# Other dense tiles, tokens paced at fewer bytes per ns in the front, and dense weights loaded two expert blocks per transfer

## The chip, the cores and the metric

The kernel runs on one core of a Trainium2 chip. The metric is the device time of one execution in microseconds (us), lower is better. A change of less than 0.3% (12 us) cannot be told from no change. Engines are named as in the profile: PE (matrix products), PEld (its weight loads), DVE (vector), ACT (activations), POOL (which issues the gathers here) and SP (which issues most transfers); a "q" behind a name is the engine's queue of instructions.

## The reference, cut to what matters

One decoder block over 1024 tokens of width 1024. A front of three attention branches, gates and projections gives `x`; then every token picks 128 of 16,384 experts (8 heads, 16 each) and mixes them:

```python
h2 = rms_norm(x, g_ffn)
q  = (hf @ w_q).reshape(T, 8, 2, 128)
sc = einsum('thpd,hpkd->thpk', q, subkeys)        # two times 128 scores a head
...                                               # top 16 of each, top 16 of the 256 sums: idx, gate
act = gelu(einsum('chkd,cd->chk', u[ic], hc))     # u, v: (16384, 1024) float32
w   = gate * act
out = einsum('chk,chkd->cd', w, v[ic])
x   = x + out
```

## The kernel before, in words

**Tiles and groups.** The 1024 tokens are eight tiles of 128. The front (`phase1`) works on four groups of two tiles, in order: norm, stick-breaking attention, dilated attention, memory attention, `gating` (24 gate blocks and their branch projections), `out_proj`, `ffn_norm`, `select` (the scores) and, as a side job, `topk`, which turns the scores of one tile at a time into expert numbers and gates. All its weights stream from HBM in blocks of 512 KB (`Weights.prepare`, tile `w`, at most four in flight).

**Two ways through the experts.** Six tiles are done by gathers (`experts`): for each token POOL issues one indirect transfer (L983) that fetches the 128 rows `[u | v]` that it picked, 8 KB a row and 1 MB a token, into one of eight buffers `uv`. DVE forms the 128 inner products (L994) against the token's row, spread over partitions by a matmul (L989), and sixteen small matmuls a token (L1015) sum the v rows into `po`. The two tiles in `DENSE` go another way: `gate_matrix` builds a full matrix of gates (128 x 128 experts a token) by one-hot products, stores it to `gd`, and at the end `dense` runs all 16,384 experts for these 256 tokens, in 128 blocks of 128 experts. A block loads `u` (512 KB, tile `ur`), `v` (512 KB, tile `vr`) and every fourth time a piece of `gd` (tile `g`, 512 KB in runs of 512 bytes); `split` makes a rounded part on ACT and the rest on DVE (L1095); 24 matmuls give the activations, ACT and DVE apply gelu and gate, and after every second block (`C = 2`) 24 matmuls bring the result through `v` and DVE adds it to `acc` (L1137). `ur`, `vr`, `uh`/`ul` and `vh`/`vl` have two buffers each.

**The order of the work** is fixed at build time by a planner at the end of `block_kernel`. The front and the dense part are one long generator (`rest`, called filler); each `yield` is a step. The planner keeps two clocks, `pe` and `dma`, in ns. A token adds `TOKEN_NS` (700) to `pe` and `TOKEN_BYTES / BW` to `dma`; a step of filler adds its matmul cost (the `cost` sums in `mm`, `mmr` and `flip`, and 50 ns) times `SLOW` (1.38 in the front, 1.1 in the dense part) to `pe` and its loaded bytes divided by `BW` to `dma`. Before each token it lays down steps of filler until `pe` has reached `dma`. Where no tile is ready (`ready` is empty) it lays down filler alone, and tokens alone where the filler is used up. A tile becomes ready when `topk` is through; a dense tile gives no tokens. All engines take their instructions in the order so laid down.

The gate matrix of a dense tile is built in the `gating` and `out_proj` steps of later groups (`stage` 1, 56 steps a group), so many of its steps with each step of the front; at `stage` 2, behind `out_proj`, all that is left of it is laid down at once. A tile takes 83 of its steps, 64 of them with work.

Of the kernel before, what the change touches and what calls it, by code (L numbers as in the profile page):

```python
# [7 lines left out]
F32 = mybir.dt.float32  # L8
# [3 lines left out]
AF = mybir.ActivationFunctionType  # L12
# [5 lines left out]
D = 1024  # L18
T = 1024
NT = T // 128  # L20
KD = D // 128
# [6 lines left out]
F32R = mybir.dt.float32r  # L28
MANUAL = dict(engines={mybir.EngineType.Activation})
GROUPS = (2, 2, 2, 2)  # L30
DENSE = (4, 5)
ND = len(DENSE)
GATES = len(GROUPS) - 1
PAUSE = 4
RG = 3
LAG = 1


BW = 375.0
SLOW = 1.38, 1.1  # L40
TOKEN_NS, TOKEN_BYTES = 700.0, 128 * 8192 + 3 * 8192.0
LEAST = 3000.0
# [32 lines left out]
def block_kernel(ctx: ExitStack, tc: tile.TileContext, io):  # L75
    nc = tc.nc
# [23 lines left out]
    cost = [0.0]  # L100
    moved = [0.0]
    table = [None]

    def bank():
        return ps.tile([128, 512], F32, name="bank")
# [8 lines left out]
    def flip(out, in_):  # L114
        cost[0] += 120
        nc.tensor.transpose(out, in_, ident)

    def actf(out, in_, f, **kw):
        s = SETS.get(f)
        if s and table[0] != s:  # L120
            nc.scalar.preload_act_table_set(s)  # L121
            table[0] = s
        nc.scalar.activation(out, in_, f, **kw)  # L123
# [111 lines left out]
    def count(ap):  # L235
        n = 4.0
        for d in ap.shape:
            n *= d
        moved[0] += n

    def load(out, src):
        count(out)
        nc.sync.dma_start(out, src)
# [486 lines left out]
    def ffn_norm(x2, n0, G, h2T):  # L730
# [26 lines left out]
        for i, h2 in enumerate(h2s):  # L757
            n = n0 + i
            if n in DENSE:
                nc.scalar.dma_start(h2d[DENSE.index(n)], h2T[:, :, i * 128:(i + 1) * 128])  # L760

            for part in range(3 if n not in DENSE else 0):
                b = gw.tile([128, D], BF, name="part", bufs=2)
# [43 lines left out]
    def topk(n0, G, scs, out):  # L807
        for i in range(G):
# [63 lines left out]
            pt = bank()  # L872
            if n0 + i in DENSE:
                flip(pt[:, 0:128], sel[:, 0, :])
# [3 lines left out]
                actf(st, pt[:, :384].rearrange("p (a b) -> p a b", a=3), AF.Copy)  # L878
                nc.scalar.dma_start(seld[DENSE.index(n0 + i)], st)
                stored.append(n0 + i)  # L880
# [143 lines left out]
    def mmr(out, lhsT, rhs, **kw):  # L1024
        cost[0] += rhs.shape[-1] / 2.4 + 3
        nc.tensor.matmul(out, lhsT, rhs, **kw)  # L1026
# [45 lines left out]
    C = 2  # L1072

    def dense():
        st = ctx.enter_context(ExitStack())
        dp = st.enter_context(tc.tile_pool(name="dp", bufs=2))
        hh = dp.tile([128, KD, TD], F32R, name="hh", bufs=1)
        hl = dp.tile([128, KD, TD], F32R, name="hl", bufs=1)
        acc = dp.tile([128, ND, D], F32, name="acc", bufs=1)
        for i in range(ND):  # L1080
            r = dp.tile([128, KD, 128], F32, name="ur")
            load(r, h2d[i])
            c = slice(i * 128, (i + 1) * 128)
            actf(hh[:, :, c], r, AF.Copy)
            nc.vector.tensor_sub(hl[:, :, c], r, hh[:, :, c])
            load(acc[:, i, :], xres[DENSE[i]])
        yield

        def split(src, name, bufs):
            r = dp.tile([128, D], F32, name=name + "r")  # L1090
            load(r, src)
            hi = dp.tile([128, D], F32R, name=name + "h", bufs=bufs)
            lo = dp.tile([128, D], F32R, name=name + "l", bufs=bufs)
            actf(hi, r, AF.Copy)
            nc.vector.tensor_sub(lo, r, hi)  # L1095
            return hi, lo

        us, vs, ws = {}, {}, {}
        gt = {}
        us[0] = split(io["uT"][0], "u", 2)  # L1100
        for c in range(128 // C):
            for x in range(C):
                e = c * C + x
                if e % 4 == 0:
                    gt = dp.tile([128, TD // 32, 4, 32], F32, name="g")
                    load(gt, gd[:, :, e:e + 4, :].rearrange("b p i t -> p b i t"))
                if e + 1 < 128:
                    us[e + 1] = split(io["uT"][e + 1], "u", 2)
                vs[x] = split(io["v"][e], "v", C)
                uh, ul = us.pop(e)  # L1110
                a = bank()
                for k in range(KD):
                    kc = slice(k * 128, (k + 1) * 128)
                    mmr(a[:, :TD], uh[:, kc], hh[:, k, :], start=k == 0, stop=False)
                    mmr(a[:, :TD], ul[:, kc], hh[:, k, :], start=False, stop=False)
                    mmr(a[:, :TD], uh[:, kc], hl[:, k, :], start=False, stop=k == KD - 1)
                w = dp.tile([128, TD], F32, name="w")
                actf(w, a[:, :TD], AF.Gelu)
                nc.vector.tensor_mul(w.rearrange("p (b t) -> p b t", t=32),
                                     w.rearrange("p (b t) -> p b t", t=32), gt[:, :, e % 4, :])  # L1120
                wh = dp.tile([128, TD], F32R, name="wh", bufs=C)
                wl = dp.tile([128, TD], F32R, name="wl", bufs=C)
                actf(wh, w, AF.Copy)
                nc.vector.tensor_sub(wl, w, wh)  # L1124
                ws[x] = wh, wl
                yield
            for i in range(ND):
                for half in range(2):
                    o = bank()
                    f = slice(half * 512, (half + 1) * 512)  # L1130
                    for x in range(C):
                        wh, wl = (z[:, i * 128:(i + 1) * 128] for z in ws[x])
                        vh, vl = (z[:, f] for z in vs[x])
                        mmr(o, wh, vh, start=x == 0, stop=False)
                        mmr(o, wh, vl, start=False, stop=False)
                        mmr(o, wl, vh, start=False, stop=x == C - 1)
                    nc.vector.tensor_add(acc[:, i, f], acc[:, i, f], o)  # L1137
                    yield
        for i in range(ND):
            nc.sync.dma_start(io["out"][DENSE[i]], acc[:, i, :])  # L1140
# [3 lines left out]
    def sides(n):  # L1144
        while n and side:
            if next(side[0], 0) == 0:
                side.pop(0)
            n -= 1
# [3 lines left out]
    def rest():  # L1152
        n0 = built = 0
        for g in range(len(GROUPS)):
            for stage in phase1(g, n0, GROUPS[g], ready):
                if stage and built < ND:

                    want = sum(n < n0 for n in DENSE)
                    while len(stored) < want:
                        sides(1)  # L1160
                    for _ in range(999 if stage == 2 else RG if g == GATES else 2):
                        if built < want:
                            built = next(gates)
                yield
            n0 += GROUPS[g]
        front.close()
        slow[0] = SLOW[1]
        yield from dense()

    filler = [rest()]  # L1170
    slow = [SLOW[0]]
    pe = dma = due = 0.0

    def fill(nside):

        c, m = cost[0], moved[0]
        if next(filler[0], 0) == 0:
            filler[0] = None
        spent = (cost[0] - c + 50) * slow[0], (moved[0] - m) / BW
        c, m = cost[0], moved[0]  # L1180
        sides(nside)
        cost[0], moved[0] = c, m
        return spent

    done = 0
    while done < NT - ND or filler[0] is not None:
        if ready:
            for _ in experts(*ready.pop(0)):

                due = max(due + LEAST, pe - LEAST)  # L1190
                while filler[0] is not None and (dma > pe or pe < due):
                    a, b = fill(1)
                    pe += a
                    dma += b
                pe += TOKEN_NS
                dma += TOKEN_BYTES / BW
            done += 1
        else:
            a, b = fill(4)
            pe += a  # L1200
            dma = max(dma + b, pe)
# [48 lines left out]
```

## Time and profile before

| | |
|---|---|
| median of 3 runs | 3950.37 us (3945.61 to 3955.39) |
| the profiled execution, its time | 3939.4 us |
| its span from first to last instruction | 3937.6 us |
| mean granted PE clock | 0.916 |
| busy share PE / DVE / ACT / POOL | 83% / 67% / 32% / 19% |
| moved by DMA | 1243.61 MB, mean 316 GB/s |
| gathers (L983) | 768 transfers, 805.36 MB of that |

The busy shares are means over stages with different limits. The second part of the page, which cuts the span into 40 slices of 98 us, and windows cut at the stages say more; they are shown with the argument. A busy digit of 9 is 90% or more, PEclk is the granted PE clock in tenths of full speed, and the DMA row is the mean busy share of the core's 16 DMA engines.

### The profile page before, as it was taken

What the parts mean: (1) busy time and instruction counts of PE and PEld (TensorE: products, weight loads), DVE (VectorE), ACT (ScalarE), POOL (GpSimd) and SP (SyncE); (2) the same over time, 40 slices, a digit from 0 to 9 for tenths busy, and PEclk for the clock granted to TensorE, in tenths of its full rate; (3) what the DMA queues carried; (4) which work ended last, traced back from release to release, by engine and by line L of the source; (5) the groups of instructions that cost most, each with busy time, mean ns of one, the idle gap of its engine ahead of it and who ended that gap; (6) DMA issues with size and microseconds to landing.
All of it is one profiled execution on the core that took longest, in us unless ns stands there. A gap on an engine that the chain in (4) does not pass through costs nothing.

```text
span 3937.6 us, 63428 instructions
## 1 busy us (share of the span) xinstructions
PE 3287.9 (83%) x23618; PEld 2552.2 (65%) x23618; DVE 2654.0 (67%) x8133; ACT 1258.3 (32%) x2518; POOL 757.0 (19%) x776
## 2 busy tenths in 40 slices
PE   7999788888768888898888898987799999999644
PEld 6889656656645565566655567876577777777411
DVE  5443696655458696554587855646988888878755
ACT  3442434420013443200145443432233433333100
POOL 0000023222222232232223210000122121111333
PEclk9999888989979999998899999998899999999865
DMA  4445479999989999999999972554799999999998
GB/s 137 127 127 173 148 307 379 371 369 402 392 338 383 394 370 358 363 396 393 403 390 378 359 291 94 186 204 149 276 343 354 369 354 358 346 332 370 367 417 364
DMA packets 293739, 1243.61 MB, mean 316 GB/s; under 512 B 31416, under 2 KB 94392, under 8 KB 191800
## 3 DMA queue, kind: packets, MB, share of 16 engines
q0 software_dynamic: 110592, 805.36, 50.7%
q1 hardware_dynamic: 157712, 394.46, 28.3%
q10 hardware_dynamic: 25128, 39.75, 2.8%
q8 instruction: 187, 3.06, 0.3%
q14 instruction: 120, 0.98, 0.1%
HBM read 1198.68 MB, written 40.76 MB: 315 GB/s over the span
## 4 chain that ended last, share of the span: by engine, by line
PE 46%; DMA 24%; DVE 18%; issue 6%; ACT 4%; POOL 2%; ACTq 0%; POOLq 0%; SPq 0%; DVEq 0%
PE bank L112 27%; PE bank L1026 12%; DMA uv<-in_uv,iT 10%; PE po L1015 6%; DVE uv L994 5%; DMA vr<-in_v 4%; DMA w<-in_w_gate 3%; POOL uv L983 2%; DMA b3d<-part 1%; DVE vl L1095 1%; DVE acc L1137 1%; DMA h2d<-big 1%; DMA w<-in_w_in 1%; DMA w<-in_w_pq 1%; DVE ul L1095 1%
## 5 line engine op out<-in xcount | busy, mean ns | idle before, releaser
L983 POOL DMA_INDIRECT uv<-in_uv,iT x768 | 756.2, 985 | 3157.8 <-PE po L1015 1192.0
L994 DVE SCALAR_TENSOR_TENSOR uv<-uv,pb 128x512 f32<-128x512 f32 x1536 | 998.7, 680 | 336.1 <-DMA uv<-in_uv,iT 289.6
L112 PE MATMUL bank<-big,w 128*128 128x256 f32 x3072 | 747.7, 395 | 92.2 <-DMA w<-in_w_gate 50.6
L112 PEld LDWEIGHTS bank<-big,w 128*128 128x128 f32 x3072 | 592.0, 197 | 221.9 <-issue 88.7
L1015 PE MATMUL po<-uv,wz 128*32 128x256 f32 x6144 | 459.0, 442 | 55.4 <-DVE wz L1006 55.0
L1015 PEld LDWEIGHTS po<-uv,wz 128*32 128x32 f32 x6144 | 202.8, 124 | 298.2 <-DVE wz L1006 121.9
L989 PE MATMUL pb<-b,which 96*128 96x512 bf16 x384 | 156.0, 429 | 232.3 <-DVE uv L994 199.7
L1026 PE MATMUL bank<-hh,ul 128*128 128x256 f32 x1024 | 296.8, 290 | 23.7 <-DVE ul L1095 23.7
L123 ACT ACTIVATE gel<-acts 128x4 f32<-128x4 f32 x192 | 38.8, 202 | 853.1 <-DVE acts L1001 842.2
L1026 PE MATMUL bank<-hh,uh 128*128 128x256 f32 x1024 | 297.2, 290 | 15.6 <-DVE pos L773 11.4
L112 PEld LDWEIGHTS bank<-w,big 128*128 128x128 f32 x2432 | 283.4, 193 | 22.2 <-issue 17.4
L1026 PE MATMUL bank<-hl,uh 128*128 128x256 f32 x1024 | 295.3, 288 | 0.0
L112 PE MATMUL bank<-w,big 128*128 128x128 f32 x2432 | 289.7, 277 | 3.7 <-DMA w<-in_w_out 3.7
L1026 PE MATMUL bank<-vh,wh 128*128 128x512 f32 x512 | 216.2, 423 | 34.0 <-ACT wh L123 31.2
L1026 PE MATMUL bank<-uv 128*128 128x256 f32 x1632 | 223.7, 294 | 15.6 <-ACT uv L123 9.0
L1026 PEld LDWEIGHTS bank<-uv 128*128 128x128 f32 x1632 | 209.2, 197 | 21.5 <-ACT uv L123 10.3
L1026 PEld LDWEIGHTS bank<-hh,ul 128*128 128x128 f32 x1024 | 201.7, 197 | 29.4 <-DVE ul L1095 26.6
L1026 PEld LDWEIGHTS bank<-hh,uh 128*128 128x128 f32 x1024 | 201.6, 197 | 24.1 <-issue 14.8
L121 ACT ACT_TABLE_LOAD x156 | 200.1, 1283 | 42.9 <-issue 14.7
L1026 PE MATMUL bank<-vh,wl 128*128 128x512 f32 x512 | 200.3, 396 | 6.3 <-DVE wl L1124 6.3
L989 PEld LDWEIGHTS <-which 96*128 96x128 bf16 x384 | 37.0, 101 | 256.8 <-issue 249.5
L1026 PEld LDWEIGHTS bank<-hl,uh 128*128 128x128 f32 x1024 | 201.7, 197 | 1.7 <-issue 1.6
(240 smaller groups left out, 5137.9 us busy)
## 6 DMA issues: line engine op xcount, KB each, us to landing
w<-in_w_in SPq DMA_DIRECT2D x136, 512.0 KB
ur<-in_uT SPq DMA_DIRECT2D x128, 512.0 KB
vr<-in_v SPq DMA_DIRECT2D x128, 512.0 KB
w<-in_w_gate SPq DMA_DIRECT2D x96, 512.0 KB
w<-in_w_pq SPq DMA_DIRECT2D x64, 512.0 KB
w<-in_w_o SPq DMA_DIRECT2D x64, 256.0 KB
w<-in_w_out SPq DMA_DIRECT2D x32, 512.0 KB
gd<-big ACTq DMA_DIRECT2D x16, 1024.0 KB
```

The costliest lines, as they stand in the source:

```text
L112: nc.tensor.matmul(out, lhsT, rhs, **kw)
L121: nc.scalar.preload_act_table_set(s)
L123: nc.scalar.activation(out, in_, f, **kw)
L983: nc.gpsimd.indirect_dma_start(out=uv, out_offset=None, in_=io["uv"], in_offset=bass.IndirectOffsetOnAxis(ap=iT[:, c, jj, i:i + 1], axis=0))
L989: nc.tensor.matmul(pb, which[:, jj].rearrange("p q s -> p (q s)"), b3[:, hh * 512:(hh + 1) * 512], start=True, stop=True)
L994: nc.vector.scalar_tensor_tensor(uv[:, f], uv[:, f], 1.0, pb, op0=OP.mult, op1=OP.mult, accum_out=parts[:, hh, i:i + 1])
L1015: nc.tensor.matmul(po[32 * k:32 * k + 32, h:h + 256], wz[:, i, :], uvs[i][:, f], start=jj == 0 and i == 0, stop=jj == QB - 1 and i == 3, s ...
L1026: nc.tensor.matmul(out, lhsT, rhs, **kw)
L1095: nc.vector.tensor_sub(lo, r, hi)
L1137: nc.vector.tensor_add(acc[:, i, f], acc[:, i, f], o)
```

## The change

- `DENSE` is (3, 5) and no longer (4, 5): tile 3 (second of the second group) goes the dense way, tile 4 (first of the third group) is gathered.
- `BW` becomes a pair: 320 bytes per ns while the front is laid down, 380 in the dense part (it was 375 throughout).
- The gate matrix moves one step with each step of `gating` and `out_proj` in any group (it was three in the last group, two in others); the rest at `stage` 2 as before.
- `u` and `v` of the dense part are stored as 64 pairs of blocks, and one transfer brings a pair: 128 rows of 8 KB, 1 MB. `raw` loads it and `split` takes one half of it. `ur` of the next pair and `vr` of the present one are loaded at the start of a pair, ahead of `g`.

```diff
-DENSE = (4, 5)
+DENSE = (3, 5)
-GATES = len(GROUPS) - 1
-RG = 3
-BW = 375.0
+BW = 320.0, 380.0
...
-        def split(src, name, bufs):
-            r = dp.tile([128, D], F32, name=name + "r")
+        def raw(src, name):
+            r = dp.tile([128, C, D], F32, name=name)
             load(r, src)
+            return r
+
+        def split(r, x, name, bufs):
             hi = dp.tile([128, D], F32R, name=name + "h", bufs=bufs)
             lo = dp.tile([128, D], F32R, name=name + "l", bufs=bufs)
-            actf(hi, r, AF.Copy)
-            nc.vector.tensor_sub(lo, r, hi)
+            actf(hi, r[:, x], AF.Copy)
+            nc.vector.tensor_sub(lo, r[:, x], hi)
             return hi, lo
...
-        us[0] = split(io["uT"][0], "u", 2)
+        ur = {0: raw(io["uT"][0], "ur")}
+        us[0] = split(ur[0], 0, "u", 2)
         for c in range(128 // C):
+            if c + 1 < 128 // C:
+                ur[c + 1] = raw(io["uT"][c + 1], "ur")
+            vr = raw(io["v"][c], "vr")
             for x in range(C):
...
-                    us[e + 1] = split(io["uT"][e + 1], "u", 2)
-                vs[x] = split(io["v"][e], "v", C)
+                    us[e + 1] = split(ur[(e + 1) // C], (e + 1) % C, "u", 2)
+                vs[x] = split(vr, x, "v", C)
...
-                    for _ in range(999 if stage == 2 else RG if g == GATES else 2):
+                    for _ in range(999 if stage == 2 else 1):
...
-        slow[0] = SLOW[1]
+        slow[0], bw[0] = SLOW[1], BW[1]
...
-        spent = (cost[0] - c + 50) * slow[0], (moved[0] - m) / BW
+        spent = (cost[0] - c + 50) * slow[0], (moved[0] - m) / bw[0]
...
-                dma += TOKEN_BYTES / BW
+                dma += TOKEN_BYTES / bw[0]
...
-        "uT": a["peer_u"][0].reshape(128, 128, KD, 128).transpose(0, 3, 2, 1).reshape(128, 128, D),
-        "v": a["peer_v"][0].reshape(128, 128, D),
+        "uT": a["peer_u"][0].reshape(64, 2, 128, KD, 128).transpose(0, 4, 1, 3, 2)
+        .reshape(64, 128, 2, D),
+        "v": a["peer_v"][0].reshape(64, 2, 128, D).transpose(0, 2, 1, 3),
```

More of the change, by code (lines that the diff above doesn't have):

```diff
@@ L1087, in dense @@
         yield
-        def split(src, name, bufs):
-            r = dp.tile([128, D], F32, name=name + "r")
+        def raw(src, name):
+            r = dp.tile([128, C, D], F32, name=name)
             load(r, src)
+            return r
+        def split(r, x, name, bufs):
             hi = dp.tile([128, D], F32R, name=name + "h", bufs=bufs)
             lo = dp.tile([128, D], F32R, name=name + "l", bufs=bufs)
-            actf(hi, r, AF.Copy)
-            nc.vector.tensor_sub(lo, r, hi)
+            actf(hi, r[:, x], AF.Copy)
+            nc.vector.tensor_sub(lo, r[:, x], hi)
             return hi, lo
         us, vs, ws = {}, {}, {}
-        gt = {}
-        us[0] = split(io["uT"][0], "u", 2)
+        ur = {0: raw(io["uT"][0], "ur")}
+        us[0] = split(ur[0], 0, "u", 2)
         for c in range(128 // C):
+            if c + 1 < 128 // C:
+                ur[c + 1] = raw(io["uT"][c + 1], "ur")
+            vr = raw(io["v"][c], "vr")
             for x in range(C):
@@ L1166, in rest @@
         front.close()
-        slow[0] = SLOW[1]
+        slow[0], bw[0] = SLOW[1], BW[1]
         yield from dense()
     filler = [rest()]
-    slow = [SLOW[0]]
+    slow, bw = [SLOW[0]], [BW[0]]
     pe = dma = due = 0.0
```

## The prediction

> **What bounds the kernel now.** I start with the 40 slices of the page, then cut windows at the places where the POOL row changes.
>
> ```profile
> span 3937.6 us, 63428 instructions
> ...
> PE   7999788888768888898888898987799999999644
> ...
> POOL 0000023222222232232223210000122121111333
> PEclk9999888989979999998899999998899999999865
> DMA  4445479999989999999999972554799999999998
> GB/s 137 127 127 173 148 307 379 371 369 402 392 338 383 394 370 358 363 396 393 403 390 378 359 291 94 186 204 149 276 343 354 369 354 358 346 332 370 367 417 364
> ```
>
> The POOL row shows where gathers run: from slice 5 to 23, none in 24 to 27, then to the end. In the gap the DMA row falls to 2 to 5 tenths and PE stands at 7 to 9. Outside it, and behind the first group, DMA is at nine tenths. So two resources take turns at being short. The windows give the amounts:
>
> ```profile
> core 0: us, PE busy (x) PEld busy (x) DVE busy (x) ACT busy (x) POOL busy (x), PEclk, DMA share, GB/s
> 0.00:505.00 505.00, 430.83 (x3291) 396.84 (x3291) 258.87 (x734) 196.29 (x402) 0.84 (x8) 0.92 0.45 142
> 505.00:2310.00 1805.00, 1504.37 (x10944) 1087.47 (x10948) 1206.04 (x4247) 551.99 (x1087) 487.04 (x508) 0.91 0.95 378
> 2310.00:2720.00 410.00, 371.73 (x2482) 320.57 (x2474) 215.47 (x823) 144.87 (x447) 3.74 (x4) 0.96 0.45 155
> 2720.00:2900.00 180.00, 127.72 (x905) 105.64 (x906) 172.24 (x545) 60.04 (x88) 25.48 (x24) 0.86 0.75 275
> 2900.00:3690.00 790.00, 741.69 (x5193) 603.92 (x5192) 664.63 (x1345) 300.23 (x473) 156.52 (x143) 0.99 0.94 354
> 3690.00:3938.00 248.00, 111.56 (x813) 37.71 (x812) 136.79 (x449) 4.93 (x24) 83.42 (x90) 0.64 0.96 394
> ```
>
> Row by row: (1) group 0, no tile ready. (2) Fronts of groups 1, 2 and the start of 3 beside 508 gathers: DMA 0.95, PE 1504 of 1805 us. (3) The rest of group 3 alone: the 512 gathers of tiles 0 to 3 are used up, PE 372 of 410 us, DMA 0.45. (4) Top-k of the last two tiles and the start of dense, DVE 172 of 180 us. (5) Dense beside 143 gathers: PE 0.94 and DMA 0.94 at once. (6) 90 gathers alone at 394 GB/s, PE 0.45. Rows 2 and 3 are what the change is about: in one the DMA engines are full, in the next they idle. That PE really waits in row 2 is in its own waits from 600 to 2300 us:
>
> ```profile
> PE pb L989 <- DVE uv L994: 74.1, 50, 8.9
> PE bank L112 <- DMA w<-in_w_gate: 50.6, 18, 8.6
> PE po L1015 <- DVE wz L1006: 30.2, 27, 8.7
> ```
>
> Token products behind late rows, and late weights: 155 us in these three alone.
>
> **The front, by the planner.** What the new constants do to the order can be worked out from the listing. Adding up the planner's own sums step by step, the filler from the first token slot to the start of dense has 440 steps with 1376 us of matmul cost (1398 with 50 ns a step) and 186 MB, or 0.133 MB per us of filler. With f us of filler to a token both clocks agree when 700 + 1380 f = 1,073,152/BW + 133,000 f/BW. BW 375: 2162 = 1025 f, f = 2.11. BW 320: 2654 = 964 f, f = 2.75. A tile has 129 slots (one sets it up), four tiles 516. Before, 516 slots take 516 x 2.11 = 1089 us of the filler, the last 309 stay alone; stepping through gives 98 steps with 333 us, which is row 3. After, 1398/2.75 = 508 slots fit. Stepping through gives the same 508 at the start of dense and never more than a few steps without a token: tile 2 ready at slot 183 (tiles 0 and 1 last to 258), tile 4 ready at 355 (tile 2 lasts to 387). So the gap goes, by an exchange of tile 4 for tile 3 that costs nothing in gathers (512 either way).
>
> Its price needs both resources over rows 2 and 3, 2215 us together.
>
> DMA: 1805 x 0.95 + 410 x 0.45 = 1899 us of engine time, unchanged. At the 0.94 that row 5 holds beside a busy PE this is 2020 us. That is the floor.
>
> PE: a token costs it (459.0 + 156.0)/768 = 0.80 us:
>
> ```profile
> L994 DVE SCALAR_TENSOR_TENSOR uv<-uv,pb 128x512 f32<-128x512 f32 x1536 | 998.7, 680 | 336.1 <-DMA uv<-in_uv,iT 289.6
> ...
> L1015 PE MATMUL po<-uv,wz 128*32 128x256 f32 x6144 | 459.0, 442 | 55.4 <-DVE wz L1006 55.0
> ...
> L989 PE MATMUL pb<-b,which 96*128 96x512 bf16 x384 | 156.0, 429 | 232.3 <-DVE uv L994 199.7
> ```
>
> The filler alone runs in row 3: 338 us of cost (with the 50 ns) in some 405 us, 1.20 of its cost, stalls included. So 1398 x 1.20 + 508 x 0.80 = 2084 us if no stall of the filler is filled by a token's matmuls, which is the pessimistic way to add. DVE is not nearer: rows 2 and 3 hold 1422 us of it. I take 2065, between 2020 and 2084 and nearer the second, as two streams that are both nearly full wait for each other. **Front: -150 us** (2215 to 2065).
>
> Bounds: below, 1899/0.95 = 2000 (-215). Above, the filler's rate in row 1, 505 us for 390 us of cost, 1.29, though that has the start in it: 1398 x 1.29 + 406 = 2209 (-6).
>
> **The gate matrix.** Work is the same; half goes from group 3 to group 2, both in the sums above. New is the dump: 56 of 83 steps go one by one, 27 remain at stage 2, in groups 2 and 3.
>
> ```profile
> L1045 DVE TENSOR_SCALAR ab<-iota,sl 128x128 f32<-128x128 f32 x256 | 86.8, 339 | 56.2 <-PE bank L112 53.8 <-DMA sl<-seld 2.4
> ...
> L1047 DVE TENSOR_SCALAR ab<-iota,sl 128x128 f32<-128x128 f32 x256 | 71.2, 278 | 0.0
> ```
>
> A step is two of each on DVE, 1.23 us; 27 (some idle) make at most 33 us in which no token is laid down. Eight `uv` buffers at 1805/508 = 3.55 us a token cover 28 us of gathers. What sticks out is 5 us a dump: **+10** (0 to +66, if nothing covered it). SP's loads queue behind nothing new here; the two 1 MB stores a quarter tile from ACT move along, 8 MB of them from the empty stretch to a full one, in the DMA sum already.
>
> **The dense part.** Eight more slots than before lie in it (266 for 258, by stepping), two of them (98 for 96) behind its last block. Six beside dense, PE-bound, at 0.80: +5; two in the tail at 248/96 = 2.6: +5. Top-k of tile 6 now has one side step a filler step, so 20 more steps of dense start beside it; row 4 is DVE-bound either way and only exchanges order: 0. BW 380 for 375 moves the ratio by 1%, in these counts.
>
> Of the transfers the page's issues, and the queues (packets, MB, share of the engines' time) from 2950 to 3650 us:
>
> ```profile
> ur<-in_uT SPq DMA_DIRECT2D x128, 512.0 KB
> vr<-in_v SPq DMA_DIRECT2D x128, 512.0 KB
> ```
>
> ```profile
> q1 hardware_dynamic: 54300, 116.42, 47.2%
> q0 software_dynamic: 17856, 130.03, 45.9%
> ```
>
> The waits (us in total, times, longest) of ACT in the same stretch, of SP from 2900 to 3690:
>
> ```profile
> ACT uh L123 <- DMA ur<-in_uT: 37.6, 17, 8.6
> ACT vh L123 <- DMA vr<-in_v: 37.4, 26, 4.3
> ```
>
> ```profile
> SPq L243 <- DVE ul L1095: 401.6, 97, 9.1
> ```
>
> Pairs halve the issues, 256 to 128, but SP is not short: it waits 401.6 us for a split to free `ur`. On the engines, q1 moves 116.42 MB in 0.472 x 700 = 330 us, 352 GB/s; q0 (8 KB rows) 130.03 MB in 321 us, 405 GB/s. Were the 134 MB of pairs to go from the one rate to the other, 49 us of DMA time would be saved at most; much of q1's loss is `g`'s short runs, which stay. PE idles 790 - 742 = 48 us in row 5 in all, so the gain ends there: -40. Against it stands latency: a pair of `ur` and `vr` is 2 MB that SP can issue only about one pair time ahead (790/58 = 13.6 us) and that needs 2.1/(0.1664 MB per us, q1's mean) = 12.6 us, where before 1 MB had the same lead. Splits now read a half only when all has come. I take **+5** (-40 to +60, a waiting ACT costing what it does now again: 37.4 + 37.6 with some hidden).
>
> The Trainium skill, "DMA: Bandwidth & Descriptors", section "Anatomy of one DMA", says that a transfer's semaphore fires only when its last byte is confirmed in place, which speaks against pairs: by it the first half comes later by the second half's 0.5 MB, 3.2 us by q1's mean rate, and 64 pairs would lose 205 us if nothing lay ahead. The row of ACT's `vr` waits, 37.4 us in 26, shows that most loads do lie ahead.
>
> **Sum.** 3939.4 - 150 + 10 + 10 + 5 = 3814 on the profiled execution, which stands 11 us under the median of the runs shown; on that scale **3825**.
>
> **The rivals.**
>
> *Better overlap.* Tokens fill all stalls of the filler and DMA holds 0.95: front 2000, dense gains 40: 3939 - 215 + 20 - 40 + 11 = 3715. For it: row 5 shows 0.94 on both at once. Against: the front's chains through ACT and DVE are longer. PEclk is 0.91 in row 2 and 0.99 in row 5; the PE work of rows 2 and 3 at 0.97 would be 1504 x 0.91/0.97 + 372 x 0.96/0.97 = 1779 us, far from binding. The Trainium skill, "TensorE: Matmul & The Clock Gate", Part 1, says that the clock is halved after an idle window of some 3.4 us and released by sustained work; the trace agrees (0.64 in the tail with PE at 0.45), and by it the fuller front runs at the better clock, which would carry this rival.
>
> *Chain-bound front.* Filler keeps the pace of row 1, 1.29: front 2209, the total 3939 - 6 + 25 + 11 = 3969 at worst, 3886 to 3955 for 1.23 to 1.28. For it: row 2 has stretches where neither PE nor DMA is full (slice 11 at 338 GB/s, slice 15 at 358, PE 8 tenths in both). Against: row 3.
>
> *Dense starved, slower.* `ur` and `vr` of a pair, and `g` behind them (2.6 MB, 15.8 us of q1's mean, against 13.6), come late and PE stops at each pair. A stop of 2 us more a pair than my +5 is 64 x 2 = 128 and brings no change; from there it decides. At 4 us: 3825 + 256 = 4081. For it: landings of `vr` are 4% of the span (some 150 us) in the chain that ended last:
>
> ```profile
> PE bank L112 27%; PE bank L1026 12%; DMA uv<-in_uv,iT 10%; PE po L1015 6%; DVE uv L994 5%; DMA vr<-in_v 4%; DMA w<-in_w_gate 3%; POOL uv L983 2%; DMA b3d<-part 1%; DVE vl L1095 1%; DVE acc L1137 1%; DMA h2d<-big 1%; DMA w<-in_w_in 1%; DMA w<-in_w_pq 1%; DVE ul L1095 1%
> ```
>
>  Against: 48 us of PE idle in row 5 says most lateness is absorbed, and the doubled buffers hold two pairs.
>
> **How the numbers follow.** Forecast (3770 to 3885) 0.62; better overlap 0.13; chain-bound 0.16, of it 0.10 faster, 0.04 the same, 0.02 slower; starved 0.09, of it 0.02 the same, 0.07 slower. Within 0.3% is 12 us, about what a measurement here can tell. Faster 0.85, same 0.06, slower 0.09. The range 3735 to 3915 leaves out half of the better overlap and the far ends of the other two.
>
> **What would show it.** POOL without the four empty slices; DMA at 0.9 or more from 500 us to the end; PE about 0.9 and PEclk 0.94 or more there; dense starting near 2570 in place of 2720, its stage 780 to 810 us; q1's packets fewer by some 16,000 to 32,000 if rows go as 8 KB. I am wrong if the DMA share in the front falls under 0.88 (chain-bound), if ACT's waits for `vr` exceed 150 us with PE idle over 100 us in dense (starved), or if gathers still pause for want of a tile.

## The result, and the profile after

The changed kernel takes 3861.03 us (median of 4, 3856.79 to 3870.02), the kernel before beside it 3952.88: a ratio of 0.9773, interval 0.9749 to 0.9796, 92 us less. The forecast was 3825, the range 3735 to 3915. The mechanism is the one forecast, its size about seven tenths of it: the sum said 125 us less; the medians fell by 92, the spans of the two profiled executions by 83.

The slices of the changed kernel's page:

```profile
span 3855.0 us, 63108 instructions
...
PE   7999789898789989888899898877798999999644
...
POOL 0000022222122222112222221120121121121332
PEclk9999889999899989999999999888899999999755
DMA  3334479889899978999898899887798989999898
GB/s 141 128 127 170 161 291 380 317 351 376 346 357 380 377 280 331 365 380 360 319 381 351 333 364 368 327 318 282 275 357 323 386 335 371 358 353 357 354 417 358
```

The POOL row has no empty stretch any more behind slice 4; one slice, 27, is a zero, where the front ends. But the DMA row does not stand at 9 throughout: 7 and 8 come back again and again, at 275 to 358 GB/s. In windows cut at the start of dense (2605) and the same stages as before (PE, PEld, DVE, ACT and POOL busy with counts, then PEclk, DMA share, GB/s):

```profile
505.00:2605.00 2100.00, 1834.55 (x13312) 1401.10 (x13313) 1390.79 (x5009) 682.96 (x1512) 486.44 (x506) 0.94 0.89 351
2605.00:2810.00 205.00, 149.82 (x1056) 119.20 (x1056) 188.34 (x580) 65.39 (x99) 29.11 (x26) 0.86 0.73 278
2810.00:3605.00 795.00, 738.91 (x5144) 604.66 (x5142) 660.33 (x1355) 290.29 (x467) 156.22 (x146) 0.97 0.90 352
3605.00:3855.00 250.00, 112.47 (x817) 37.69 (x813) 138.66 (x452) 4.93 (x24) 84.71 (x91) 0.59 0.96 395
```

The front takes 2100 us in place of 2215 with 506 gathers in it; the start of dense 205 for 180; dense and the tail are as they were. So the front gave 115, and 32 came back between the start of dense and the end. The last row of each kernel's `acc` additions tells where that is (first and last start), before and after:

```profile
L1137 DVE TENSOR_TENSOR acc<-acc,bank x256: 662/681/690, 2746.7 to 3688.8; 128x512 f32<-128x512 f32 x128
```

```profile
L1141 DVE TENSOR_TENSOR acc<-acc,bank x256: 665/682/690, 2641.5 to 3596.6; 128x512 f32<-128x512 f32 x128
```

From the start of dense (2719 and 2605) to the first addition 27.5 and 36.5 us, from first to last 942 and 955, behind it to the end 249 and 258.

### The profile page after: what moved, and what is told of

The parts are those of the page before. It is cut to its first block, busy times and chain, and to the rows that moved or that the text cites. A ratio compares the mean times of both kernels' runs of the same rounds, so it can differ in the third digit from the quotient of the medians.

```text
span 3855.0 us, 63108 instructions
## 1 busy us (share of the span) xinstructions
PE 3263.3 (85%) x23618; PEld 2556.4 (66%) x23618; DVE 2641.3 (69%) x8133; ACT 1241.1 (32%) x2506; POOL 757.3 (20%) x776
## 3 DMA queue, kind: packets, MB, share of 16 engines
q1 hardware_dynamic: 139280, 394.45, 27.6%
## 4 chain that ended last, share of the span: by engine, by line
PE 48%; DMA 22%; DVE 13%; issue 11%; ACT 3%; POOL 2%; ACTq 0%; POOLq 0%; SPq 0%; DVEq 0%
PE bank L110 24%; PE bank L1024 17%; DMA uv<-in_uv,iT 13%; PE po L1013 6%; DMA w<-in_w_gate 4%; DVE uv L992 3%; POOL uv L981 2%; DMA b3d<-part 1%; DMA w<-in_w_in 1%; ACT e L121 1%; PE pb L987 1%; PE bank L114 1%; DMA w<-in_w_out 1%; DVE ul L1096 1%; ACT L119 1%
## 5 line engine op out<-in xcount | busy, mean ns | idle before, releaser
L110 PE MATMUL bank<-big,w 128*128 128x256 f32 x3072 | 729.5, 391 | 56.1 <-DMA w<-in_w_gate 38.9
L1013 PE MATMUL po<-uv,wz 128*32 128x256 f32 x6144 | 444.9, 431 | 56.3 <-DVE wz L1004 56.2
L1013 PEld LDWEIGHTS po<-uv,wz 128*32 128x32 f32 x6144 | 199.0, 121 | 283.8 <-DVE wz L1004 107.3
L987 PE MATMUL pb<-b,which 96*128 96x512 bf16 x384 | 142.7, 417 | 180.0 <-DVE uv L992 160.6
L121 ACT ACTIVATE big<-bank 128x128 f32<-128x128 f32 (+3 forms) x406 | 124.2, 385 | 335.3 <-PE bank L110 288.7
L1024 PE MATMUL bank<-vl,wh 128*128 128x512 f32 x512 | 206.4, 403 | 0.0
```

What stands on the lines that cost most here:

```text
L987: nc.tensor.matmul(pb, which[:, jj].rearrange("p q s -> p (q s)"), b3[:, hh * 512:(hh + 1) * 512], start=True, stop=True)
L1013: nc.tensor.matmul(po[32 * k:32 * k + 32, h:h + 256], wz[:, i, :], uvs[i][:, f], start=jj == 0 and i == 0, stop=jj == QB - 1 and i == 3, s ...
```

## The experiments

The first four ran on a chip where the kernel before takes 4049.33 us; nearly all of that excess is in the front (e3_pairs, whose front is that of the kernel before, starts dense at 2809 us there for 2719). Times of whole kernels are therefore compared by ratio there. The others ran on chips where it takes 3948.21 and 3955.69.

**The change taken apart.** Three kernels, each the kernel before with one part of the change.

```diff
-BW = 375.0
+BW = 320.0, 380.0        # e1_pace: and the lines that use it, nothing else
```

> The kernel before with the pace alone (BW 320 in the front, 380 in dense); dense tiles 4 and 5, single-block loads and the old rate of the gate matrix stay. Theory (the pace closes the gap): by the planner's sums 508 token slots lie in the front and tile 3 is ready well before tile 2 is used up, so nothing is lacking without the exchange of tiles; the gap at 2310 to 2720 us goes, dense starts at 2600 to 2625 as after the change, and the time is 3850 to 3880. Rival (the exchange of tiles is needed, since both gate matrices then fall into group 3's full front): dense starts at 2650 or later, time 3900 or more. Rival (the pairs bring part): time above that of the changed kernel by 20 or more.

Measured: 0.9734 (0.971 to 0.9758), 3941.39 for 4049.33. The pace alone does all of it. Dense starts at 2696 us on this chip, and that and the time would by their absolute figures be the rival's; those figures were set from runs on a faster chip, and on another, below (f1_pace5), the same kernel starts dense at 2606 and takes 3856.96.

```diff
-DENSE = (4, 5)
+DENSE = (3, 5)           # e2_tiles: nothing else
```

> The kernel before with dense tiles 3 and 5 alone; pace 375, single-block loads, gate matrix two and three steps at a time. Theory (the pace is what counts): tiles 0 and 1, 2 are used up before tile 4 is ready, so two pauses of gathers in place of one, 29 and 90 steps by the planner's sums against 107 before; time 3935 to 3975, no gain. Rival (the exchange brings the gain by itself): 3870 or less.

Measured: 0.9987 (0.9967 to 1.0007). Its slices show the one gap split in two, at slice 19 and at 25 to 27:

```profile
POOL 0000022222223222222012222000111212112232
PEclk9989889889989999899989999998899999999756
DMA  4335489889999998899758888454789999989998
```

For the third, `raw` and `split` of the changed kernel and its storage of `u` and `v` were put into the kernel before (e3_pairs).

> The kernel before with the pairs of blocks per transfer alone; tiles, pace and gate matrix as before. Theory (PE bounds the dense stage, late loads are absorbed): within 12 us of the kernel before; ACT's waits for ur and vr shrink and its waits for PE grow by as much. Rival (weights come sooner, PE idles less): 20 to 40 us faster. Rival (starved, half a transfer can't be used): 15 to 60 us slower. The changed kernel's dense part, from its start to its last block, was 29 us longer (1000 for 971); if the pairs are the cause, this kernel shows it as well.

Measured: 0.999 (0.9974 to 1.0006). In its dense part from 3000 to 3750 us ACT waits 3.1 us for `ur`:

```profile
ACT w L123 <- PE bank L1026: 199.7, 45, 7.6
...
ACT uh L123 <- DMA ur<-in_uT: 3.1, 1, 3.1
```

and in e2_tiles, with single blocks, in the same stretch:

```profile
ACT w L123 <- PE bank L1026: 119.6, 40, 6.3
...
ACT uh L123 <- DMA ur<-in_uT: 38.5, 11, 8.6
...
ACT vh L123 <- DMA vr<-in_v: 33.4, 27, 2.8
```

The pairs remove 70 us of waiting for landings, and ACT waits 80 us more for PE in its place: the old waits were under PE's cover. The time is the same, so neither the starved nor the better case holds.

The ratio of the pace alone, 0.9734, was under that of the whole change, so both were timed once more on one chip:

> The pace alone again (BW 320 and 380, dense tiles 4 and 5, single blocks), now on the same chip as the changed kernel. Theory (exchange of tiles, pairs and the gate matrix's new rate are worth nothing): the same as the changed kernel within 8 us. Rival (they cost something, as the earlier ratio of 0.973 beside 0.978 hints): 10 to 25 us faster than the changed kernel.

> The changed kernel, as the base for the kernel with the pace alone: 0.978 of the kernel before.

Measured: 0.9761 (0.9736 to 0.9786) and 0.9753 (0.9729 to 0.9776), 3856.96 and 3863.05 us. The exchange of tiles, the pairs and the new rate of the gate matrix are together worth nothing that can be told.

**What the front is made of.** First without its tokens:

```diff
-        if ready:
+        if ready and ready[0][0] < 6:      # e5_alone: tiles 0, 1, 2, 4 dropped
+            ready.pop(0)
+            done += 1
+        elif ready:
```

> The changed kernel without the gathers of tiles 0, 1, 2 and 4: these four tiles' expert sums are left out, everything else stays, so groups 1 to 3 of the front run alone. In the changed kernel the front took 2100 us (505 to 2605) with 508 tokens. Theory (the front's own pace plus the tokens' PE time, sum of both): the front alone takes 2100 - 508 x 0.80 = 1690 us, 1.21 of its cost of 1398. Rival (DMA contention is what stretches it): the front alone takes 1550 us or less. By stretch: theory expects attention at 1.25 of its cost or more and gating at 1.1 or less, since the changed kernel's DMA share is 0.73 to 0.87 in attention and 0.95 to 1.01 in gating.

Measured: the start of dense at 2188 us, so the front alone takes 1683 us, 1.20 of its cost. By stretch of group 2 (attention; gating with `out_proj`; the rest), columns as above:

```profile
1010.00:1310.00 300.00, 255.13 (x1735) 202.23 (x1735) 143.15 (x465) 109.49 (x245) 0.00 (x0) 0.92 0.27 81
1310.00:1480.00 170.00, 168.98 (x992) 152.81 (x991) 66.60 (x251) 42.31 (x126) 0.00 (x0) 1.00 0.52 171
1480.00:1590.00 110.00, 97.36 (x477) 82.31 (x477) 64.73 (x286) 34.21 (x104) 0.00 (x0) 0.92 0.54 183
```

Against the planner's cost of the same steps, added up from the listing by stretch (224, 182 and 76 us), that is 1.34, 0.93 and 1.45; in groups 1 and 3 attention is 1.36 and 1.32, gating 0.99 and 0.88. One factor of 1.38 fits none but attention. It is PE that is busy in gating (0.99), while in attention even alone it idles 45 of 300 us, with DMA at 0.27; the waits that the trace lists for it there are for DVE and ACT.

Then with tokens of half the bytes, beside the changed kernel on the same chip:

```diff
-                nc.gpsimd.indirect_dma_start(out=uv, out_offset=None, in_=io["uv"],
+                nc.gpsimd.indirect_dma_start(out=uv[:, :D], out_offset=None, in_=io["uh"],
...
-                                f = slice(D + 256 * k, D + 256 * k + 256)
+                                f = slice(256 * k, 256 * k + 256)      # e6_half
```

> The changed kernel again, beside the three that follow. It gives their base: 0.977 of the kernel before.

> The changed kernel with gathers of 4 KB rows: only u is fetched, v is left out, and the sums through v use the products in the u half, so a token moves 0.5 MB in place of 1 MB while PE, DVE, ACT and the order of the work stay. The front alone took 1683 us (pace and PE only), beside tokens 2100; PE time of 508 tokens is 406. Theory (attention is bound by PE and its chains, gating and the rest in part by DMA): attention of groups 1 to 3 keeps its 310 + 360 + 370 us within 5%, gating with out_proj falls from 200 + 220 + 230 to about 615, the rest from 415 to 380; the front 2030 to 2060. Rival (DMA contention everywhere): attention falls by 8% or more and the front is under 1980. Rival (all PE and chains): the front stays above 2085. The tail, 90 gathers at 2.6 us each, should go to about half.

Measured: a0_after 0.9781 (0.9752 to 0.9811). Group 2 in the same three stretches, a0_after:

```profile
1140.00:1500.00 360.00, 318.02 (x2508) 227.84 (x2507) 262.08 (x917) 168.94 (x312) 89.87 (x92) 0.92 0.85 331
1500.00:1720.00 220.00, 198.52 (x1401) 164.85 (x1400) 133.01 (x487) 40.04 (x132) 49.19 (x52) 0.97 0.96 383
1720.00:1870.00 150.00, 119.83 (x714) 93.30 (x713) 102.50 (x423) 38.66 (x118) 26.31 (x28) 0.87 0.91 353
```

and e6_half:

```profile
1120.00:1480.00 360.00, 319.38 (x2522) 231.37 (x2521) 262.19 (x923) 170.33 (x314) 89.41 (x92) 0.94 0.61 205
1480.00:1680.00 200.00, 196.17 (x1412) 163.05 (x1411) 136.35 (x505) 42.58 (x142) 49.37 (x52) 1.00 0.82 286
1680.00:1820.00 140.00, 110.54 (x669) 85.28 (x670) 92.92 (x372) 35.35 (x106) 26.60 (x28) 0.89 0.70 246
```

Attention takes 360 us with 331 GB/s and with 205: half the token's bytes change nothing there (305, 360 and 380 us in the three groups become 315, 360 and 370). Gating falls by 20 to 0.98 PE busy, the rest by 10. In all the front falls from 2103 to 2014, 16 below the range set for it. So of the 420 us that 508 slots add to the front alone, 331 stay at half the bytes (0.65 us a token) and 89 go with the other half of the bytes. That holds as far as the front alone, measured on the other chip, is the same on this one. It was not run on both; group 0, which has no gathers beside it, takes the same time on both (the first gather is issued at 520 us in e1_pace and at 518 in a0_after).

What a token costs PE in the front can be read off the changed kernel's trace, by the two lines of a token's matmuls (L1013, eight a token, and L987, one for two tokens), in the front and in the tail (first L1013, then L987; PE and PEld busy with counts, PEclk, DMA share, GB/s):

```profile
505.00:2605.00 2100.00, 263.21 (x4000) 123.21 (x4000) 0.94 0.89 351
3605.00:3855.00 250.00, 86.14 (x772) 33.03 (x768) 0.59 0.96 395
```

```profile
505.00:2605.00 2100.00, 85.80 (x250) 24.68 (x251) 0.94 0.89 351
3605.00:3855.00 250.00, 26.33 (x45) 4.66 (x45) 0.59 0.96 395
```

That is 0.70 us a token in the front (0.53 and 0.17) and 1.2 in the tail, where the granted clock is 0.59. The 0.80 of the prediction and of the expectations is the mean over all stages. So the 1690 set for the front alone came near its 1683 in part by luck: the 420 us are 0.83 a slot, 0.70 of it PE's own time and the rest waiting. The tail of e6_half did not halve as expected: from the last `acc` addition to the end it still takes 194 us for 258, 2.0 us for each of 98 slots, so at half the bytes something else than the bytes is near.

**Another split of the tokens.** If attention has DMA to spare, tokens should lie there and not in gating:

```diff
-BW = 320.0, 380.0
+BW = 360.0, 380.0        # e7_phase
...                       # phase1, groups 1 to 3
+            slow[0] = 1.4     # at its start
+            slow[0] = 1.0     # ahead of gating
+            slow[0] = 1.2     # ahead of ffn_norm
```

> The changed kernel with SLOW by stretch of the front in place of 1.38: attention 1.4, gating and out_proj 1.0, the rest 1.2, and BW 360 in the front, so that all 516 slots still fit. Alone, attention took 1.32 to 1.47 of its cost, gating with out_proj 0.88 to 0.99. By the planner's sums attention gets 88 + 97 + 122 slots for 72 + 79 + 99, gating 38 + 43 + 42 for 51 + 59 + 58. Theory (gating is DMA-bound, attention is not): gating falls to the sum of its own pace and 0.8 us a token, about 72 us less, attention pays 57 x 0.8 = 46; 20 to 40 us faster than the changed kernel (0.968 to 0.972 of the kernel before). Rival (attention with more tokens is DMA-bound as well): same or slower than the changed kernel, 0.975 or more.

Measured: 0.9794 (0.9763 to 0.9825), not faster than a0_after, and the front is longer, dense starting at 2658 for 2608. That is the time the rival set; its mechanism shows in group 1 alone. Attention and gating of groups 1 and 2:

```profile
505.00:840.00 335.00, 286.46 (x2271) 207.90 (x2270) 246.68 (x873) 138.92 (x265) 92.15 (x96) 0.92 0.92 365
840.00:1040.00 200.00, 172.37 (x1082) 140.37 (x1082) 78.17 (x243) 19.61 (x48) 34.02 (x36) 0.95 0.85 326
...
1185.00:1550.00 365.00, 310.99 (x2493) 218.85 (x2493) 268.10 (x932) 164.97 (x302) 96.58 (x102) 0.92 0.91 358
1550.00:1770.00 220.00, 201.52 (x1338) 168.67 (x1338) 121.56 (x448) 43.13 (x139) 38.81 (x41) 0.96 0.86 332
```

In a0_after attention of group 1 took 305 us with 78 gathers: 18 more cost 30 us, 1.7 a token and not 0.8. In group 2, 10 more cost 5 us (365 for 360), so the price is not the same everywhere. What the theory lacks is the gain: gating took 200 us with 51 gathers and takes 200 with 36, at a DMA share of 0.85 for 1.00, and in group 2 220 with 52 and with 41. So gating with tokens isn't simply bound by the bytes of its tokens. (The 1.47 and the 97 slots for 79 of the expectation, both for group 2, count steps into the wrong stretch; by stretch it is 1.34, and 109 slots for 89.) What keeps it at 200 to 220 us, against 150 to 170 alone, stays open.

**The dense part's pace.**

```diff
-BW = 320.0, 380.0
+BW = 320.0, 420.0        # e8_dense
+BW = 320.0, 460.0        # f3_dense460
```

> The changed kernel with BW 420 for 380 in the dense part, which moves 44 of the 98 slots of the tail beside dense blocks by the planner's sums. Theory (dense is PE-bound at a DMA share of 0.90, a token costs 0.8 us there and 2.6 us in the tail): 44 x 1.8 = 79 us less at most; as the DMA share would reach 0.99, 35 to 65 us less, 0.961 to 0.968 of the kernel before. Rival (dense is as DMA-bound as the tail): within 12 us of the changed kernel.

> The changed kernel with BW 460 for 380 in the dense part; by the planner's sums 7 slots are left behind the last block, where BW 420 left 54 and 380 left 98. At 420 the dense stage moved 379 GB/s at a DMA share of 0.96 and a token cost 1.4 us there. Theory (dense is DMA-bound from there, the next 47 tokens cost what they cost in the tail, 2.6 us): within 12 us of the kernel with 420, 0.960 to 0.966 of the kernel before. Rival (still PE-bound, 1.4 us a token or less): 40 to 55 us faster than it, 0.950 to 0.954.

Measured: 0.9635 (0.9594 to 0.9677), 3802.53 us, inside the range of the first theory; and 0.9573 (0.9548 to 0.9597), 3787.83 us beside 3863.05 of the changed kernel, the fastest of all. The `acc` additions of f3_dense460 end 26 us before its end, where the changed kernel has a tail of 258:

```profile
L1141 DVE TENSOR_TENSOR acc<-acc,bank x256: 666/682/690, 2651.2 to 3759.9; 128x512 f32<-128x512 f32 x128
```

From the start of dense to the last addition e8_dense takes 1053 us for a0_after's 989, 1.5 us for each of 44 tokens moved, f3_dense460 1144 for 990, 1.7 for each of 91, where a token in the tail takes 2.6. The second 47 cost 1.9 each by the difference, so both theories of f3_dense460 miss: the price climbs, and stays under the tail's. DMA is full there, 800 us of f3_dense460's dense stage:

```profile
2800.00:3600.00 800.00, 705.85 (x5096) 557.05 (x5095) 661.91 (x1501) 256.79 (x425) 209.68 (x194) 0.94 1.00 396
```

Last, the same without exchange and pairs (the kernel before with `BW = 320.0, 440.0`):

> The kernel before with the pace alone, 320 in the front and 440 in the dense part; no exchange of tiles, single blocks. If the exchange and the pairs do nothing, this is as fast as the changed kernel with 420 to 460 in the dense part: 0.955 to 0.965 of the kernel before, the fastest of all with the least change. Rival (pairs matter once DMA is full in dense): 0.968 or more.

Measured: 0.9668 (0.9642 to 0.9693), 3823.22 us, between what its two expectations set (0.965 and 0.968), so it decides for neither. It is a little behind e8_dense (the intervals overlap) though it has fewer slots left behind the last block (31 for 54), and 35 us behind f3_dense460. From 2850 to 3600 us its ACT waits 142 us for landings,

```profile
ACT uh L123 <- DMA ur<-in_uT: 94.4, 20, 12.6
...
ACT vh L123 <- DMA vr<-in_v: 48.1, 34, 2.8
```

f3_dense460's 12.2 for `ur`, none of note for `vr`:

```profile
ACT uh L121 <- DMA ur<-in_uT: 12.2, 6, 4.9
```

So the pairs, worth nothing at 380, look worth something like 20 us once DMA is full in the dense stage. f4_pace440 differs from its neighbours also in `BW` (440 for 420 and 460), in the dense tiles and in the rate of the gate matrix, so neither the size nor the cause is settled.

## Why the prediction was right, and where it was off

- *The gap goes.* Right. The 508 slots fit, dense starts without a pause of tokens before it, and the pace alone does it. The exchange of tile 4 for tile 3, which the working put beside it, is not needed: with tiles 4 and 5 dense, tile 3 is ready in time as well (f1_pace5 starts dense at 2606 us).
- *The front's size.* This is the term that was mis-sized: -150 in the working, -115 measured. The filler alone was put at 1.20 of its cost, 1678 us, and measured 1683. The step that failed is the choice of 2065 between the sum of 2084 and the DMA floor of 2020, on the ground that the sum was pessimistic. The front took 2100, but that the sum came so near is in part luck, as two errors in it cancel. A token's PE time of 0.80 us is the mean over all stages; in the front it is 0.70, so the sum with the front's own price is 1683 + 355 = 2038. And the sum leaves out waits: some 62 us more are measured. At half the bytes the tokens add 331 us for 348 of PE time (0.69 a token in e6_half), so hardly any stall of the filler is filled; the other half of the bytes adds 89. The floor at a share of 0.94 is not reached; the share is 0.89, because attention, half of the front, takes as long at half the bytes, with DMA at 0.85 (a0_after and e6_half). The sign of being wrong, a share under 0.88, was missed by 0.01.
- *The gate matrix.* +10 for the two dumps; lies inside the front's number and can't be told in it. f1_pace5, in which both gate matrices are through before `stage` 2 comes, has the same time.
- *The dense part.* +15 in the working, +32 measured: 9 before the first addition, 13 between the additions, 10 behind them. Most of it goes with the pace and not with the pairs: from the start of dense to the end f1_pace5 takes 1240 us, the changed kernel 1250, e3_pairs 1224 and the kernel before 1219. Priced at zero was the top-k of tile 6, one side step a filler step, now running beside the first dense blocks with eight slots left over. That this is the cause was not tried by itself.
- *Pairs.* +5 between -40 and +60: right near zero. q1's packets fell from 157712 to 139280, 18,432 fewer, which is what one packet for a row of 8 KB in place of two of 4 KB (16,384) and one less on each of 16 engines for 128 fewer transfers (2048) would give. The rule of the Trainium skill ("DMA: Bandwidth & Descriptors", "Anatomy of one DMA"), in a section on transfers that gpsimd issues, that the semaphore fires only with the last byte was no cost to these, which SP issues: ACT's waits for `ur` and `vr` shrank.
- *The better overlap.* Not reached, though the clock rose: PEclk is 0.94 in the front for 0.91 beside gathers before, 0.97 in gating with PE at 0.90 and 0.59 in the tail with PE at 0.45. That agrees with the rule of the Trainium skill ("TensorE: Matmul & The Clock Gate", Part 1) that idling lowers the clock and sustained work releases it.
- *Chain-bound front.* Half right: attention alone takes 1.32 to 1.36 of its cost with neither PE nor DMA full; gating, at 0.88 to 0.99, makes up for it. One reading under this rival was wrong and would have spoken for it: in slice 11 of the profile before PE stands at 6 tenths, not 8.

## What to carry to other kernels

Where a planner deals out two streams, set its pace so that neither runs out before the other, and check both ends: here the front's gap was worth 2.4%, and the tail behind the dense part, which the change left as it was, another 1.8% by one number. To forecast such a mix, add the time of the one stream alone to the busy time of the other on the engine they share, priced in the same stage, and expect waits for the shared DMA on top (here 62 us on 2038); don't take stalls for free room. A transfer made larger shortens waits that may be covered, and then the time does not show it.

## What the runs showed of the hardware that was not expected

One program takes different times on different chips, and by stage: the front of the kernel with the pace alone takes 2191 us on one (505 to 2696) and 2101 on another (505 to 2606), while from there to the end it takes 1249 and 1240. And a token's time does not halve with its bytes when it runs alone behind the dense part: 2.6 us a slot at 8 KB rows and 2.0 at 4 KB, counting from the last `acc` addition to the end (258 and 194 us) with 98 slots in it.
